# The attention scores' third product: both maps side by side, each in one half of the rows

## The chip, the cores and the metric

The kernel runs on one core of a Trainium2 chip. The metric is the device time of one execution in microseconds, as the median of several runs. The profile is one execution, recorded instruction by instruction. Five engines work in parallel, each through its own list in a fixed order: TensorE (PE, with its weight loads as PEld), VectorE (DVE), ScalarE (ACT), GpSimd (POOL) and SyncE (SP), which issues most transfers.

## The reference, cut to what matters

One layer of a hybrid encoder over 2048 tokens of width 1024: a combined input projection, differential attention and a gated delta rule as two branches, their gated merge, an output projection, and a mixture of experts. The change lies in the attention alone:

```python
DA_HEADS, DA_QK_DIM, DA_V_DIM = 4, 64, 128      # two maps of 64 channels per head
def probs(qm, km):
    s = jnp.einsum('bhqd,bhkd->bhqk', qm, km).astype(jnp.float32) * scale + bias
    return jax.nn.softmax(jnp.where(allowed, s, NEG_INF), axis=-1)
a = probs(qblk[..., 0, :], k1) - lam * probs(qblk[..., 1, :], k2)
return jnp.einsum('bhqk,bhkd->bhqd', a.astype(v.dtype), v)
```

So each head has two maps, and each map's scores contract over only 64 channels. `allowed` lets a query see the keys of its own chunk of 64 and of all chunks before it.

## The kernel before

Stages follow one another: conditioning and input projection (phase 1), the delta rule with the output gates, the attention with the branches' merge (phase 2), the output projection with routing (phase 3), the experts (phase 5). In most products each float32 operand is split into a high part that TensorE multiplies in its fast float32r form and a low part (what is left), so that a product takes three matmuls: high by high, high by low, low by high.

The attention goes by units `att(p, h, qt, ...)`: one head `h` and one tile of 128 queries `qt`, 64 units in three passes (`qt` 0 to 7, 8 to 11, 12 to 15). A unit does, for each of two maps `m` and each chunk `ch` of up to 512 keys:

- L979: queries' high part times keys. The contraction of 64 is doubled to 128 rows: the tile `K` holds a map's high keys in rows 0 to 63 and its low keys in rows 64 to 127, and `qd` holds the high queries twice. One matmul over 128 rows gives high by high plus high by low.
- L980: the third product, `ql` (the low queries, also held twice) times the same `K` tile, again over 128 rows, added in the same PSUM bank (tag `sc`, three banks).
- L982: VectorE reads the bank, adds the distance bias and keeps the minimum (tile `mx`), into the score rows `sp`.

After a map's chunks come the exponential on ScalarE (L987), and after both maps the combination (L994). Later come the transposes of the probabilities (`tr`, L1002), their copies (`aT`, L1004) and the products with the values (`av`, L1006).

The units are generators that `pipeline` starts one per turn; older ones go on to their next `yield 1`. Between the attention's units stand gate units (`pg`, L548 to L550, in the first pass) and merge units (`y`, L867 to L869). What order each engine runs comes from the framework's scheduler, which weaves these units together, so TensorE's list holds score products, transposes, value products and merge products in turn. The loads go through SyncE: `kv_load` (L946: per chunk one transfer for the high and one for the low keys, both maps in each; L948 for the values) and `q_load` (L956, L957: four transfers per head and 512 queries).

Of the kernel before, what the change touches and what calls it, by code (L numbers as in the profile page):

```python
# [9 lines left out]
F32 = mybir.dt.float32  # L10
F32R = mybir.dt.float32r
# [8 lines left out]
P = 128  # L20
# [23 lines left out]
# gates of the last slab that wait for the attention, and the units of it that they come before  # L44
# [16 lines left out]
def pipeline(units, old_first=False):  # L61
    """each turn starts a unit and runs the older ones to their next "yield 1"; "yield 0" lets the others in between"""
    active, more = [], True
    units = iter(units)
    while active or more:
        g = next(units, None)
        more = more and g is not None
        turn, active = ([] if g is None else [g]) + active, []
        if old_first:
            turn.reverse()  # L70
        while turn:
            again = []
            for g in turn:
                r = next(g, None)
                if r is not None:
                    (active if r else again).append(g)
            turn = again
        if old_first:
            active.reverse()


class K:
# [59 lines left out]
    # ---------------------------------------------------------------- phase 1  # L142
    def phase1(self, late):
# [13 lines left out]
        with ExitStack() as ctx:  # L157
# [25 lines left out]
            def load_x(p):  # L183
                """two tiles of x, normalized"""
# [7 lines left out]
                # the second pair is waited for: its first tile by itself  # L192
# [100 lines left out]
            # per-partition gain of q: both maps' 64 channels  # L293
# [7 lines left out]
            # a head's scores are in units of its slope, a power of two, until the bias is on  # L301
# [254 lines left out]
    def gates_and_gdn(self, ctx, sm, ps, hxp, hh, hl):  # L556
# [33 lines left out]
        # softplus(x) = max(x, 0) + log1p(e), e = exp(-|x|); log1p(e) = ln(u) e / (u - 1), u = 1 + e  # L590
# [96 lines left out]
        def scan(t):  # L687
# [6 lines left out]
            for b in range(4):  # L694
                pb, o = slice(32 * b, 32 * b + 32), 32 * (b % 2)
                nc.sync.dma_start(T[pb, :, o:o + 32], TB[t, :, b].rearrange("h r c -> r h c"))
                nc.sync.dma_start(U[pb, :, o:o + 32], UB[t, :, b].rearrange("h r c -> r h c"))
                # the zero quarter of each pair of blocks
                G.memset((U if b % 2 else T)[pb, :, 32 - o:64 - o], 0.0)
# [11 lines left out]
            # inverse of the unit triangular matrix, block doubling 32 -> 64 -> 128  # L711
# [32 lines left out]
            # recurrence over tiles of 128 tokens  # L744
# [76 lines left out]
    # ---------------------------------------------------------------- branch merge  # L821
    def merge_setup(self, ctx, ps):
# [6 lines left out]
        def load_o(s, n, h):  # L829
            """a head's output of a slab, as parts"""  # L830
            hi = c.tile([P, TS], F32R, tag="oh", name=f"h{n}{s}{h}", bufs=NOT)
            lo = c.tile([P, TS], F32R, tag="ol", name=f"l{n}{s}{h}", bufs=NOT)
            raw = lo.bitcast(F32)
            nc.sync.dma_start(raw, d[n][h, :, s * TS:(s + 1) * TS])
            A.copy(hi, raw)
            (V if s == NS - 1 else G).tensor_tensor(out=lo, in0=raw, in1=hi.bitcast(F32), op=ALU.subtract)
            ot[n, s, h] = hi, lo
# [47 lines left out]
    # ---------------------------------------------------------------- phase 2  # L885
    def phase2(self, cm, late):
# [3 lines left out]
        with ExitStack() as ctx:  # L890
# [8 lines left out]
            # ---- constants  # L899
# [16 lines left out]
            # distances of keys from queries, the last chunk's first half of queries doesn't see its second half of keys  # L916
# [9 lines left out]
            # ---- attention  # L926
            kv, qs = {}, {}

            def kv_tiles(p, h, n):
                """the first 512 keys' tiles come last: their memory is free first"""  # L930
# [6 lines left out]
            def kv_load(p, h, n):  # L937
                """the keys and values of a head, n chunks"""
# [4 lines left out]
                for s in range(n):  # L943
                    sl = slice(s * TS, (s + 1) * TS)
                    for j, nm in ((0, "k_hi"), (1, "k_lo")):
                        nc.sync.dma_start(Kt[s].bitcast(F32)[64 * j:64 * j + 64],  # L946
                                          d[nm][h].rearrange("(m p) t -> p m t", m=2)[:, :, sl])
                    nc.sync.dma_start(Vt[s], vs[:, 4 * s:4 * s + 4, :])  # L948

            def q_load(h, s):  # L950
                qd = ah.tile([P, 2, TS], F32R, tag="qd", bufs=NQ, name=f"qd{h}{s}")
                ql = ah.tile([P, 2, TS], F32R, tag="ql", bufs=NQ, name=f"ql{h}{s}")
                sl = slice(s * TS, (s + 1) * TS)
                for t, nm in ((qd, "q_hi"), (ql, "q_lo")):
                    src = d[nm][h].rearrange("(m p) t -> p m t", m=2)[:, :, sl]
                    nc.sync.dma_start(t.bitcast(F32)[0:64], src)  # L956
                    nc.sync.dma_start(t.bitcast(F32)[64:128], src)  # L957
                # numerators, their first maps' sums and sums of squares, of four query tiles
# [6 lines left out]
            def att(p, h, qt, sp_pool, w):  # L965
# [6 lines left out]
                sp = []  # L972
                for m in range(2):
                    b = sp_pool.tile([P, w], F32, tag="sp", name=f"sp{h}_{qt}_{m}")
                    mx = sm.tile([P, 5], F32, tag="mx", name=f"mx{h}_{qt}_{m}")
                    for ch in range(nch):
                        k0, n = ch * 512, min(512, nk - ch * 512)
                        pt = ps.tile([P, 512], F32, tag="sc", name=f"sc{h}_{qt}_{m}_{ch}", bufs=PSA[0])
                        PE.matmul(pt[:, :n], qd[:, m, q0], Kt[ch][:, m, 0:n], start=True, stop=False)  # L979
                        PE.matmul(pt[:, :n], ql[:, m, q0], Kt[ch][:, m, 0:n], start=False, stop=True)  # L980
                        mo = S - nk + k0
                        V.tensor_tensor_reduce(out=b[:, k0:k0 + n], in0=pt[:, :n], in1=Mt[:, mo:mo + n], op0=ALU.add,  # L982
                                               op1=ALU.min, scale=SLOPES[h], scalar=3e38, accum_out=mx[:, ch:ch + 1])
# [5 lines left out]
                    sp.append(b)  # L989
# [23 lines left out]
                # out = o / l1, rms-normalised; a mean square beyond float32 gives 0, as its rsqrt does  # L1013
# [27 lines left out]
            def units():  # L1041
# [14 lines left out]
                for i, (p, h, qt) in enumerate(todo):  # L1056
                    wn = TS * (p + 2)
                    if wn != w:
# [4 lines left out]
                        # the first pass's lies where the merge's tiles come, which are not to be loaded before  # L1063
# [31 lines left out]
    # ---------------------------------------------------------------- phase 3  # L1095
    def phase3(self, cm):
# [5 lines left out]
        with ExitStack() as ctx:  # L1102
# [72 lines left out]
            def outp(i, s, j):  # L1175
# [29 lines left out]
                # logits of a slab by columns: 36 rows of the weights' first parts, 36 of their second  # L1205
# [44 lines left out]
    # ---------------------------------------------------------------- phase 4  # L1250
    def route_consts(self, ctx):
# [3 lines left out]
        # descending weights 8..1, expert number, iota over slots columns and partitions  # L1255
# [14 lines left out]
        # an expert's share of the schedule, in half blocks: one, and one more for each of these its rank lies below  # L1270
# [17 lines left out]
    def first(self, sm, x, n, tg):  # L1288
        """one-hot of the first maximum over the last axis of x, and the maximum"""
# [16 lines left out]
    def route_a(self, sm, t0, t1):  # L1306
# [13 lines left out]
        # the two best experts of every group  # L1320
# [13 lines left out]
        # their weights  # L1334
# [10 lines left out]
    def route_b(self, c, sm, wk, wp, ps):  # L1345
# [8 lines left out]
        # loads of the experts, as a column and in every row  # L1354
# [6 lines left out]
        # positions of the assignments within their experts  # L1361
# [4 lines left out]
        # rank of an expert: experts in falling order of load, ties in expert order  # L1366
# [9 lines left out]
        # expert of a rank  # L1376
# [8 lines left out]
        # the schedule: NBLK blocks in rank order, what goes beyond an expert's share after them  # L1385
# [12 lines left out]
        # base, share and first further block of an expert in one number  # L1398
# [37 lines left out]
        # token and weight of a slot; the weight in two parts  # L1436
# [26 lines left out]
        # the other experts' weights are read after the first rows  # L1463
# [11 lines left out]
        # blocks beyond the schedule: how many, and each expert's range of them  # L1475
# [6 lines left out]
        def weights():  # L1482
# [5 lines left out]
            # halved, for the tanh form of silu  # L1488
# [5 lines left out]
    def spots(self, wk, wp, g, act=False):  # L1494
        """one-hot rows of the places in their blocks, of eight tiles of assignments"""
# [16 lines left out]
    def rows_of(self, pool, pt, nm):  # L1512
        """rows to gather and to add to, from a table of token numbers counted from 1, 0 where there is none"""
# [11 lines left out]
    # ---------------------------------------------------------------- phase 5  # L1525
    def phase5(self):
# [3 lines left out]
        with ExitStack() as ctx:  # L1530
# [15 lines left out]
            def chunks(e, i):  # L1546
                """loads of an expert's weights, two rows of 128 of w1 and w3 or one of w2 at a time"""
# [13 lines left out]
            def split(more):  # L1561
                """the next loaded weights' parts, and another load"""
# [14 lines left out]
            def block(i, more, gi, si, wt, nm):  # L1577
# [26 lines left out]
                # silu(a)*b, as a*(1 + tanh(a/2))*b/2; the half goes into the weight  # L1604
# [26 lines left out]
            def half(i, more, gi, si, wt, nm):  # L1631
                """a block of up to 64 tokens: their two parts side by side, the products with the first part of the
                weights in the upper and in the lower half, added afterwards"""
# [63 lines left out]
            def behind(g):  # L1697
                """the older block's products come before this one's rows"""
# [30 lines left out]
            with tc.For_i(0, n, 1) as i:  # L1729
                # the block's number, its expert, its tokens and their weights  # L1730
# [68 lines left out]
```

## Time and profile before

| | |
|---|---|
| median of 3 runs | 3081.26 us (3079.08 to 3086.68) |
| profiled execution, its span | 3079.4 us |
| TensorE busy over the span | 2844.8 us (92%) |
| attention stretch (first to last score product and its tail) | 1292 to 1824 us |
| TensorE busy in that stretch | 495.02 of 532 us |

The page gives no device time of the profiled execution other than its span, which lies 1.9 us below the median. A matmul's listed duration runs from its start to its last result and is longer than its share of the engine, since the next one starts before it has ended; so starts are compared with starts.

### The profile page before, as it was taken

Reading aid. Unit: us, or ns where it says so; the run is one execution under the profiler, and the core shown is the slowest. Engines: PE = TensorE matmul, PEld = TensorE weight load, DVE = VectorE, ACT = ScalarE, POOL = GpSimd, SP = SyncE. Lnnn points to the kernel's source line nnn. Section 1 sums busy time; section 2 is a strip of 40 time slices with the busy share of each in tenths; the row PEclk is TensorE's granted clock in tenths of the full one; section 3 lists DMA queues with packets and bytes.
Section 4 is the critical chain, followed back from the end, with each engine's and each line's share of the span. In section 5 each row is a group of like instructions: output and inputs, shape, how many; then the busy total and the mean of one; then the engine's idle time right before and its main releaser. Section 6 shows DMA issues by size and latency. Waiting matters only on the chain. (4 is left out here: it accounts for less than half of the span.)

```text
span 3079.4 us, 43963 instructions
## 1 busy us (share of the span) xinstructions
PE 2844.8 (92%) x14845; PEld 2294.6 (75%) x14845; DVE 2079.0 (68%) x4804; ACT 1332.7 (43%) x2409; POOL 837.8 (27%) x614
## 2 busy tenths in 40 slices
PE   6999999999999999999899999997799899999897
PEld 4888778777877777777788787786577677667675
DVE  7567669985276443377757655676867767886876
ACT  4512223333322333377555543221545545554554
POOL 2200000000221222001342324221544545543553
PEclk9999999999999999999999999998799999999998
DMA  6334652221554664585676647532978888886895
GB/s 224 119 86 117 202 182 80 79 67 53 165 144 130 185 179 147 149 200 148 167 179 171 168 110 235 195 144 103 324 240 259 260 258 292 294 291 217 271 312 148
DMA packets 426245, 561.20 MB, mean 182 GB/s; under 512 B 56520, under 2 KB 240920, under 8 KB 426016
## 3 DMA queue, kind: packets, MB, share of 16 engines
q1 hardware_dynamic: 340560, 440.87, 46.4%
q10 hardware_dynamic: 73744, 75.53, 7.3%
q0 software_dynamic: 11712, 41.95, 5.8%
q8 instruction: 119, 1.95, 0.3%
q14 instruction: 110, 0.90, 0.1%
HBM read 436.06 MB, written 122.18 MB: 181 GB/s over the span
## 5 line engine op out<-in xcount | busy, mean ns | idle before, releaser
L1570 DVE TENSOR_TENSOR low<-raww,hiw 128x1024 fp32r<-128x1024 f32 x288 | 434.4, 1554 | 46.8 <-ACT hiw L1568 44.2
L1568 ACT CAST hiw<-raww 128x1024 fp32r<-128x1024 f32 x384 | 378.8, 1048 | 153.6 <-PE py L1624 67.7
L1570 POOL TENSOR_TENSOR low<-raww,hiw 128x1024 fp32r<-128x1024 f32 x96 | 263.2, 2771 | 118.9 <-ACT hiw L1568 112.7
L982 DVE CUSTOM_DVE_ANT_0 sp<-sc,M 128x512 f32<-128x512 f32 (+1 forms) x320 | 183.6, 604 | 53.1 <-PE sc L980 52.0
L548 PE MATMUL pg<-hh,ghi 128*128 128x512 f32 x512 | 210.5, 411 | 2.5 <-ACT ghi L539 2.5
L332 PE MATMUL mma<-whi,hh 128*128 128x512 f32 x512 | 208.5, 407 | 2.4 <-ACT hh L248 1.0
L550 PE MATMUL pg<-hh,glo 128*128 128x512 f32 x512 | 208.3, 407 | 0.0
L549 PE MATMUL pg<-hl,ghi 128*128 128x512 f32 x512 | 208.0, 406 | 0.0
L334 PE MATMUL mma<-whi,hl 128*128 128x512 f32 x512 | 202.8, 396 | 0.6 <-DVE hl L249 0.6
L333 PE MATMUL mma<-wlo,hh 128*128 128x512 f32 x512 | 202.1, 395 | 0.4 <-DVE wlo L255 0.4
L987 ACT ACTIVATE sp<-sp,mx 128x128 f32<-128x128 f32 (+15 forms) x128 | 153.7, 1201 | 46.4 <-DVE mx L985 40.7
L1006 PEld LDWEIGHTS av<-V,aT 128*128 128x128 f32 x1088 | 140.2, 196 | 34.6 <-ACT aT L1004 26.7
L1006 PE MATMUL av<-V,aT 128*128 128x128 f32 x1088 | 151.6, 284 | 13.9 <-ACT aT L1004 12.7
L255 POOL TENSOR_TENSOR wlo<-raw,whi 128x512 fp32r<-128x512 f32 x12 | 16.9, 1428 | 533.0 <-ACT whi L254 533.0
L342 PE MATMUL mmb<-hh,whi 128*128 128x512 f32 x384 | 155.3, 404 | 5.4 <-ACT whi L254 5.4
L344 PE MATMUL mmb<-hh,wlo 128*128 128x512 f32 x384 | 151.1, 393 | 0.6 <-POOL wlo L255 0.4
L343 PE MATMUL mmb<-hl,whi 128*128 128x512 f32 x384 | 150.3, 391 | 0.0
L979 PE MATMUL sc<-K,qd 128*128 128x512 f32 (+1 forms) x320 | 132.1, 416 | 14.7 <-DVE mx L982 10.9
L1623 PE MATMUL py<-hiw,dh 128*128 128x512 f32 x272 | 115.1, 423 | 20.4 <-ACT dh L1614 20.3
L1597 PE MATMUL pb<-low,xh 128*128 128x512 f32 x272 | 112.7, 414 | 18.3 <-DVE low L1570 10.7
L1579 POOL DMA_INDIRECT x<-h,sgi x34 | 63.6, 1872 | 230.1 <-PE tx L1586 132.7
L1597 PE MATMUL pa<-low,xh 128*128 128x512 f32 x272 | 111.3, 409 | 11.9 <-DVE low L1570 11.9
(555 smaller groups left out, 7522.3 us busy)
## 6 DMA issues: line engine op xcount, KB each, us to landing
raww<-in_w_dram SPq DMA_DIRECT2D x384, 512.0 KB
mw<-in_w_ada_dram SPq DMA_DIRECT2D x64, 256.0 KB
gate<-gt ACTq DMA_DIRECT2D x64, 256.0 KB
g<-gate SPq DMA_DIRECT2D x64, 256.0 KB
graw<-in_w_in_dram SPq DMA_DIRECT2D x52, 256.0 KB
raw<-in_w_in_dram SPq DMA_DIRECT2D x22, 512.0 KB
K<-k_hi SPq DMA_DIRECT2D x36, 256.0 KB
K<-k_lo SPq DMA_DIRECT2D x36, 256.0 KB
```

The lines of the kernel that those rows point to most:

```text
L332: nc.tensor.matmul(pt[:, :n], a, his[k][:, :n], start=(k == 0), stop=False)
L333: nc.tensor.matmul(pt[:, :n], a, los[k][:, :n], start=False, stop=False)
L334: nc.tensor.matmul(pt[:, :n], b, his[k][:, :n], start=False, stop=(k == KT - 1))
L342: nc.tensor.matmul(pt, a, hh[s][:, k, :], start=(k == 0), stop=False)
L548: nc.tensor.matmul(pt, hi[:, k, :], hh[:, k, :], start=(k == 0), stop=False)
L549: nc.tensor.matmul(pt, hi[:, k, :], hl[:, k, :], start=False, stop=False)
L550: nc.tensor.matmul(pt, lo[:, k, :], hh[:, k, :], start=False, stop=(k == KT - 1))
L982: V.tensor_tensor_reduce(out=b[:, k0:k0 + n], in0=pt[:, :n], in1=Mt[:, mo:mo + n], op0=ALU.add, op1=ALU.min, scale=SLOPES[h], scalar=3e38, ...
L1006: PE.matmul(av[:, :P], aT[:, k * P:(k + 1) * P], Vt[k4 // 4][:, k, :], start=(k4 + k == 0), stop=(k4 + k == qt))
L1568: A.copy(hi, raw)
L1570: on.tensor_tensor(out=lo, in0=raw, in1=hi.bitcast(F32), op=ALU.subtract)
L1597: PE.matmul(p_, xh[:, k, :], w[i, n, k][q], start=(k == 0 and q == 0), stop=False)
```

## The change

The keys' tile is laid out anew: for map 0 the high keys stand in rows 0 to 63 and the low ones in rows 64 to 127, as before; for map 1 the high keys stand in rows 64 to 127 and the low ones in rows 0 to 63. The low queries are held once, map 0 in rows 0 to 63 and map 1 in rows 64 to 127. The third product is then a matmul over 64 rows: low queries by high keys alone, the upper rows for map 0, the lower rows for map 1 (low by low is left out of the sum). The two maps of a chunk are emitted together: both first products, both third products, both VectorE passes. Both maps' exponentials stand after the last chunk. Each key transfer is split by map, and the low queries need one transfer in place of two. Comments were removed from the file, so that lines behind the change stand about six lower: L980 and L984 are now the first and third product, L987 the VectorE pass, L1008 and L1012 the transposes and value products.

```diff
                 for s in range(n):
                     sl = slice(s * TS, (s + 1) * TS)
-                    for j, nm in ((0, "k_hi"), (1, "k_lo")):
-                        nc.sync.dma_start(Kt[s].bitcast(F32)[64 * j:64 * j + 64],
-                                          d[nm][h].rearrange("(m p) t -> p m t", m=2)[:, :, sl])
+                    for m in range(2):
+                        for j, nm in ((m, "k_hi"), (1 - m, "k_lo")):
+                            nc.sync.dma_start(Kt[s].bitcast(F32)[64 * j:64 * j + 64, m, :],
+                                              d[nm][h, 64 * m:64 * m + 64, sl])
...
-                ql = ah.tile([P, 2, TS], F32R, tag="ql", bufs=NQ, name=f"ql{h}{s}")
+                ql = ah.tile([P, TS], F32R, tag="ql", bufs=NQ, name=f"ql{h}{s}")
...
+                nc.sync.dma_start(ql.bitcast(F32), d["q_lo"][h][:, sl])
...
-                sp = []
+                sp = [sp_pool.tile([P, w], F32, tag="sp", name=f"sp{h}_{qt}_{m}") for m in range(2)]
+                mxs = [sm.tile([P, 5], F32, tag="mx", name=f"mx{h}_{qt}_{m}", bufs=6) for m in range(2)]
+                for ch in range(nch):
+                    k0, n = ch * 512, min(512, nk - ch * 512)
+                    pts = [ps.tile([P, 512], F32, tag="sc", name=f"sc{h}_{qt}_{m}_{ch}", bufs=PSA[0]) for m in range(2)]
+                    for m, pt in enumerate(pts):
+                        PE.matmul(pt[:, :n], qd[:, m, q0], Kt[ch][:, m, 0:n], start=True, stop=False)
+
+                    for m, pt in enumerate(pts):
+                        r = slice(64 * m, 64 * m + 64)
+                        PE.matmul(pt[:, :n], ql[r, q0], Kt[ch][r, m, 0:n], start=False, stop=True)
+                    mo = S - nk + k0
+                    for m, pt in enumerate(pts):
+                        V.tensor_tensor_reduce(out=sp[m][:, k0:k0 + n], in0=pt[:, :n], in1=Mt[:, mo:mo + n], op0=ALU.add,
+                                               op1=ALU.min, scale=SLOPES[h], scalar=3e38, accum_out=mxs[m][:, ch:ch + 1])
                 for m in range(2):
-                    b = sp_pool.tile([P, w], F32, tag="sp", name=f"sp{h}_{qt}_{m}")
-                    mx = sm.tile([P, 5], F32, tag="mx", name=f"mx{h}_{qt}_{m}")
-                    for ch in range(nch):
-                        k0, n = ch * 512, min(512, nk - ch * 512)
-                        pt = ps.tile([P, 512], F32, tag="sc", name=f"sc{h}_{qt}_{m}_{ch}", bufs=PSA[0])
-                        PE.matmul(pt[:, :n], qd[:, m, q0], Kt[ch][:, m, 0:n], start=True, stop=False)
-                        PE.matmul(pt[:, :n], ql[:, m, q0], Kt[ch][:, m, 0:n], start=False, stop=True)
...
+                    b, mx = sp[m], mxs[m]
```

TensorE's list in the third pass before the change, at query tile 13 of the third head (a row reads line, operation, output tile with query tile, map and chunk in its name, then stationary and moving operand in the trace's order, and the size):

```order
L979 MATMUL sc_13_0_0_17119<-K_16332,qd_16346 128x512
L980 MATMUL sc_13_0_0_17119<-K_16332,ql_16347 128x512
L979 MATMUL sc_13_0_1_17123<-K_16326,qd_16346 128x512
L980 MATMUL sc_13_0_1_17123<-K_16326,ql_16347 128x512
L979 MATMUL sc_13_0_2_17127<-K_16328,qd_16346 128x512
L980 MATMUL sc_13_0_2_17127<-K_16328,ql_16347 128x512
L1002 MATMUL tr_12_0_17162<-ident,sp_12_0_16955 128x128 x3
L979 MATMUL sc_13_0_3_17131<-K_16330,qd_16346 128x256
L980 MATMUL sc_13_0_3_17131<-K_16330,ql_16347 128x256
```

The same place after the change:

```order
L980 MATMUL sc_13_0_0_17177<-K_16374,qd_16396 128x512
L980 MATMUL sc_13_1_0_17178<-K_16374,qd_16396 128x512
L984 MATMUL sc_13_0_0_17177<-K_16374,ql_16397 128x512
L984 MATMUL sc_13_1_0_17178<-K_16374,ql_16397 128x512
L980 MATMUL sc_13_0_1_17185<-K_16368,qd_16396 128x512
L984 MATMUL sc_13_0_1_17185<-K_16368,ql_16397 128x512
L1008 MATMUL tr_12_0_17218<-ident,sp_12_0_17011 128x128 x2
L980 MATMUL sc_13_1_1_17186<-K_16368,qd_16396 128x512
L984 MATMUL sc_13_1_1_17186<-K_16368,ql_16397 128x512
L1008 MATMUL tr_12_0_17218<-ident,sp_12_0_17011 128x128 x2
```

Only the first chunk's two third products (L984) stand next to each other. From the second chunk on, each stands alone, with transposes or the other map's first product behind it. Over the whole list the 320 third products form 259 groups without another product between them: 199 of one, 59 of two and one of three, so that 60 of the 160 pairs stand together; the 60 hold 27,520 of the 69,632 columns that one map's third products have in all. Behind 108 of the groups stands a 512-wide or narrower float32r product, behind 151 a transpose or value product.

SyncE's list at the first head's loads, before and after the change (a piece of the difference, names of buffers kept):

```order
L956 DMA qd_12033<-q_hi 64x2x512
L957 DMA qd_12033<-q_hi 64x2x512
L956 DMA ql_12034<-q_lo 64x2x512
L957 DMA ql_12034<-q_lo 64x2x512
L946 DMA K_12031<-k_hi 64x2x512
L946 DMA K_12031<-k_lo 64x2x512
```

The low queries' two transfers become one of 128 rows (L959), and each key transfer becomes two of half the size (L948 in the new file).

## Rows read from the trace of the kernel before

**Rows 1.** The page's head and busy times: engine, busy us (share of the span), instructions.

```profile
span 3079.4 us, 43963 instructions
PE 2844.8 (92%) x14845; PEld 2294.6 (75%) x14845; DVE 2079.0 (68%) x4804; ACT 1332.7 (43%) x2409; POOL 837.8 (27%) x614
```

**Rows 2.** Busy time by stretch, the attention: us, each engine's busy us (instructions), clock.

```profile
core 0: us, PE busy (x) PEld busy (x) DVE busy (x) ACT busy (x) POOL busy (x), PEclk, DMA share, GB/s
1292.00:1824.00 532.00, 495.02 (x2920) 416.01 (x2921) 375.09 (x1267) 322.02 (x701) 130.38 (x103) 0.97 0.66 167
```

**Rows 3.** Instruction groups of TensorE in 1292 to 1824: busy, mean | idle before, releasers.

```profile
L1006 PE MATMUL av<-V,aT 128*128 128x128 f32 x1034 | 144.7, 285 | 13.9 <-ACT aT L1004 12.7 <-ACT av L1009 0.9
L979 PE MATMUL sc<-K,qd 128*128 128x512 f32 (+1 forms) x320 | 132.1, 416 | 14.7 <-DVE mx L982 10.9 <-DMA qd<-q_hi 1.5 <-DMA K<-k_lo 0.9
L980 PE MATMUL sc<-K,ql 128*128 128x512 f32 (+1 forms) x320 | 119.5, 380 | 2.1 <-DMA ql<-q_lo 2.1
```

**Rows 4.** TensorE in order of time, attention: start, duration, line, operation, rows*columns, size.

```profile
1704.90 0.39 PE L980 MATMUL sc<-K,ql 128*128 128x512 f32 x1
1705.13 0.38 PE L1002 MATMUL tr<-ident,sp 128*128 128x128 f32 x2
1705.27 0.48 PE L979 MATMUL sc<-K,qd 128*128 128x512 f32 x1
1705.58 0.40 PE L980 MATMUL sc<-K,ql 128*128 128x512 f32 x1
```

**Rows 5.** TensorE in order of time, delta rule: eight 64-row products among gate products.

```profile
1070.95 0.40 PE L550 MATMUL pg<-hh,glo 128*128 128x512 f32 x1
1071.28 0.68 PE L737 MATMUL p<-sU,nw 64*64 64x64 f32 x8
1071.88 0.50 PE L548 MATMUL pg<-hh,ghi 128*128 128x512 f32 x1
1072.22 0.40 PE L549 MATMUL pg<-hl,ghi 128*128 128x512 f32 x1
```

**Rows 6.** TensorE in order of time, experts: four 64-row transposes, four 128-row ones behind them.

```profile
2268.91 0.40 PE L1599 MATMUL pb<-hiw,xl 128*128 128x512 f32 x1
2269.24 0.46 PE L1674 MATMUL th<-ident,ha 64*128 64x64 f32 x4
2269.64 0.66 PE L1586 MATMUL tx<-ident,x 128*128 128x128 f32 x4
2270.05 0.48 PE L1597 MATMUL pa<-hiw,xh 128*128 128x512 f32 x1
2270.37 0.39 PE L1597 MATMUL pa<-low,xh 128*128 128x512 f32 x1
```

**Rows 7.** TensorE in order of time, experts: 128-row products that use half of the columns.

```profile
2238.90 0.40 PE L1657 MATMUL pb<-hiw,xh 128*128 128x512 f32 x1
2239.13 0.39 PE L1657 MATMUL pa<-low,xh 128*64 128x512 f32 x1
2239.37 0.39 PE L1657 MATMUL pb<-low,xh 128*64 128x512 f32 x1
```

**Rows 8.** TensorE in order of time, delta rule: 32-row products in different parts of the array.

```profile
951.67 0.19 PE L724 MATMUL pb<-A,sT 32*32 32x32 f32 x1
951.68 0.19 PE L717 MATMUL pa<-sU,nw 32*32 32x32 f32 x1
951.68 0.19 PE L726 MATMUL pb<-sT,A 32*32 32x32 f32 x1
951.71 0.19 PE L724 MATMUL pb<-A,sT 32*32 32x32 f32 x1
```

**Rows 9.** Instruction groups of VectorE in 1292 to 1824, by shape, columns as above.

```profile
L982 DVE CUSTOM_DVE_ANT_0 sp<-sc,M 128x512 f32<-128x512 f32 x224 | 147.9, 684 | 29.6 <-PE sc L980 29.0
L982 DVE DVE_READ_ACCUMULATOR2_ANT mx<- 128x1 f32 x320 | 26.1, 81 | 0.0
```

**Rows 10.** Waits of VectorE in 1292 to 1830: who for whom, us, times, longest.

```profile
DVE cf L992 <- ACT sp L987: 44.1, 27, 2.5
```

**Rows 11.** The key loads' line on SyncE: count, duration ns (min/median/max), first and last start.

```profile
L946 SPq DMA_DIRECT2D K<-k_hi x36: 573/586/1631, 1284.8 to 1763.8; - x36
L946 SPq DMA_DIRECT2D K<-k_lo x36: 574/605/807, 1285.4 to 1764.4; - x36
```

More of the change, by code (lines that the diff above doesn't have):

```diff
@@ L951, in q_load @@
                 qd = ah.tile([P, 2, TS], F32R, tag="qd", bufs=NQ, name=f"qd{h}{s}")
-                ql = ah.tile([P, 2, TS], F32R, tag="ql", bufs=NQ, name=f"ql{h}{s}")
+                ql = ah.tile([P, TS], F32R, tag="ql", bufs=NQ, name=f"ql{h}{s}")
                 sl = slice(s * TS, (s + 1) * TS)
[L954 to L957, printed above, removed]
+                src = d["q_hi"][h].rearrange("(m p) t -> p m t", m=2)[:, :, sl]
+                nc.sync.dma_start(qd.bitcast(F32)[0:64], src)
+                nc.sync.dma_start(qd.bitcast(F32)[64:128], src)
+                nc.sync.dma_start(ql.bitcast(F32), d["q_lo"][h][:, sl])
                 ob = at.tile([P, 4, P], F32, tag="ob", bufs=4, name=f"ob{h}{s}")
@@ L971, in att @@
                 nch = (nk + 511) // 512
-                sp = []
-                for m in range(2):
-                    b = sp_pool.tile([P, w], F32, tag="sp", name=f"sp{h}_{qt}_{m}")
-                    mx = sm.tile([P, 5], F32, tag="mx", name=f"mx{h}_{qt}_{m}")
-                    for ch in range(nch):
-                        k0, n = ch * 512, min(512, nk - ch * 512)
-                        pt = ps.tile([P, 512], F32, tag="sc", name=f"sc{h}_{qt}_{m}_{ch}", bufs=PSA[0])
-                        PE.matmul(pt[:, :n], qd[:, m, q0], Kt[ch][:, m, 0:n], start=True, stop=False)
-                        PE.matmul(pt[:, :n], ql[:, m, q0], Kt[ch][:, m, 0:n], start=False, stop=True)
-                        mo = S - nk + k0
-                        V.tensor_tensor_reduce(out=b[:, k0:k0 + n], in0=pt[:, :n], in1=Mt[:, mo:mo + n], op0=ALU.add,
-                                               op1=ALU.min, scale=SLOPES[h], scalar=3e38, accum_out=mx[:, ch:ch + 1])
+                sp = [sp_pool.tile([P, w], F32, tag="sp", name=f"sp{h}_{qt}_{m}") for m in range(2)]
[12 more added lines that the diff above has]
+                                               op1=ALU.min, scale=SLOPES[h], scalar=3e38, accum_out=mxs[m][:, ch:ch + 1])
+                for m in range(2):
+                    b, mx = sp[m], mxs[m]
                     if nch > 1:
@@ L988, in att @@
                                  accum_out=(l1, l2)[m][:, j:j + 1])
-                    sp.append(b)
                 yield 1
```

## The prediction

> **What bounds the kernel now.** I read the page first: TensorE is busy for 92% of the span and no other engine for more than 68% [rows 1]. Then the busy times by stretch: in the attention, the only place where the change acts, TensorE is busy for 495.0 of 532 us at a granted clock of 0.97 of full speed, VectorE for 375.1, and so 37 us of TensorE are idle [rows 2]. The groups of that stretch say where: 13.9 us before the value products, mostly for ScalarE's copies, 14.7 us before the first score product, of which 10.9 for VectorE to empty a bank, 2.1 for a load of queries [rows 3]. So TensorE's list, run in order, sets the stretch's length, and a price or gain on TensorE reaches the end nearly in full, except where it falls into those 37 us.
>
> The timeline gives the prices. A 512-wide float32r product is followed by the next instruction 0.23 us later (1704.90 to 1705.13). Two transposes and a first score product behind it take from 1705.13 to 1705.58, 0.45 us, so a 128-wide transpose costs 0.11. From one L980 to the next it is 0.68 us, which is 0.23 + 2 x 0.11 + 0.23: weaving transposes between score products costs nothing today [rows 4].
>
> **What the change takes away.** Two third products of one chunk in different halves of the rows could run at once. The trace has no pair of 64-row products like that. The nearest rows are the delta rule's 32-row ones: three products in different parts of the array start within 0.01 us, while the same line returns 0.04 us later [rows 8]. So I take side by side as true where the two follow each other directly, a gain of one product's time for the pair. But TensorE's list after the change has only 60 of 160 pairs standing together; in the other 100 a transpose, a value product or the other map's first product stands between, and TensorE runs its list in order. The 60 pairs hold 27,520 columns, which is 53.75 products of 512 at 0.23: **12.4 us taken away** (0 if they do not overlap). A third product that stands alone over 64 rows is as wide as before and saves nothing.
>
> **What the change adds on TensorE.** Every group of third products is now a visit to 64 rows among products over 128 rows, and the trace shows what such a visit costs. In [rows 5] the time from L550's start to the second product behind the visit is 1072.22 - 1070.95 = 1.27 us. The work in it is 0.23 for L550, eight 64-wide products at 0.06 (half of the 0.11 of a 128-wide one, rounded up) and 0.23 for L548: 0.94. The visit cost 0.33 us over its work: 0.10 to get in (0.33 between L550 and L737 where 0.23 is usual), about 0.10 to get out and 0.11 more on the first product behind (0.34 to the next), the rest inside. In [rows 6] it is the same with 64-row transposes and 128-row transposes behind them: 2270.37 - 2268.91 = 1.46 us, less 0.23 + 4 x 0.06 + 4 x 0.11 + 0.23 = 1.14, leaves 0.32. No idle time is listed before any of these rows; nothing is waited for. It is the rows, not the columns: products that use 64 columns and all 128 rows follow the others at 0.23 and 0.24 [rows 7], and 128-row transposes cost nothing extra [rows 4].
>
> The Trainium skill says in "TensorEngine Tiling (Array Packing)", Key Properties, that changing the tiling mode, and not just the tile within one, drains TensorE. By that, every visit drains twice, as [rows 5, 6] show; that columns alone change without any delay [rows 7] it does not separate. The page gives no duration.
>
> No row shows a 512-wide 64-row product in such a visit. From below: only the way in, 0.10 us [rows 5]. From above: the first product of the visit also starts as slowly as the first one behind it, 0.11 more, but without what was lost inside in [rows 5]: 0.40. I take 0.33, since in both kinds of visit seen, with float32r products and with transposes behind, it comes out at 0.33 and 0.32. The list after the change has 259 groups: 259 x 0.33 = **85.5 us added** (26 to 104).
>
> **What hides some of it.** Where TensorE waits today, a slower TensorE waits less: at most the 37 us of [rows 2]. In the dense parts VectorE offers no cover: a chunk takes it 0.684 + 0.081 = 0.77 us [rows 9], while TensorE's share of a chunk goes from 0.68 [rows 4] to 0.68 + 0.33 = 1.01. And the waits for loads and for the first chunks of a unit stay. I take a third, **12 us** (0 to 37).
>
> **Edits costed at nothing.** Both exponentials now stand at the unit's end, so the combination waits longer for ScalarE; VectorE waits 44.1 us there today [rows 10], and the cover is the next unit's or merge's products on TensorE, which need none of it. If that cover were gone, at most the length of one such wait, 2.5 us, would fall on a unit. Both score rows are claimed at the unit's start, the second one up to four chunks (3 us) sooner; no wait for them is among the waits of today. SyncE issues 72 more key transfers and 16 fewer query transfers of 0.6 us each [rows 11], 34 us over a stretch of 532, most in bursts of 4 to 8 more transfers per head, 2.4 to 4.8 us; heads are loaded one ahead, and TensorE waits 0.9 us for keys today [rows 3]. Only the first head is not loaded ahead: 2 key issues more and 1 query issue less before its first chunk, under 1 us, while gate products still run. VectorE's and ScalarE's work is the same in count and size.
>
> **Sum.** -12.4 + 85.5 - 12 = +61 us. On the profiled span of 3079.4 that is 3140; the median lies 1.9 above that span, so I predict **3142 us**, 2% slower, all of it within the attention stretch, which grows from 532 to about 593 us. What follows starts later and is otherwise as before.
>
> **Rivals.**
> 1. *The visit is cheap for these products*, because a 512-wide product gives the engine time to get the next weights ready, and just the way in of 0.10 us stays: +26 - 12.4 = +13.5 us, about 3095. For it: the rows inside the visits of [rows 5, 6] are short ones. Against: the delay behind the visit is seen on 512-wide products with 512-wide ones following.
> 2. *Faster.* The visit costs nothing, and pairs overlap. It gives -12.4 us, about 3069, as the list stands; it decides below a price of 12.4 / 259 = 0.048 us a visit, and to be faster by 9 us (0.3%, about what a measurement of this kernel can tell from no change) below 0.013. For it: [rows 8]. Against: 0.10 in on every visit seen, before any other part. If all 160 pairs overlapped and no visit cost anything it would be 69,632 columns, 136 products x 0.23 = -31 us, about 3050; the list excludes it. The Trainium skill's page "TensorE: Matmul & The Clock Gate", Part 3, lets products in distinct row groups run at once, some 4 ns apart, which is this case for the pairs that stand together.
> 3. *Worse.* The pairs do not overlap, the visit costs 0.40 and nothing is hidden: +104, about 3185. For it: no 64-row pair is in the trace. Against: TensorE's waits must shrink somewhat.
> 4. *The waits hide much more:* all 37 us vanish: +85.5 - 12.4 - 37 = +36, about 3117. For it: the waits for the copies and banks are those a slower TensorE loses. Against: [rows 9], and loads.
>
> **Chances.** The forecast with its own range, 3125 to 3180: 0.64. Rival 4's end, 3105 to 3125: 0.14. Rival 1, 3090 to 3105: 0.06. Rival 3, above 3180: 0.05. No change within 0.3%, a visit of about 0.05 us: 0.06. Rival 2: 0.05. So slower has 0.89, the same 0.06, faster 0.05. The range of 3102 to 3178 leaves out rivals 1 to 3 and no change, about 0.2.
>
> **What would show it.** In the profile after: from a first score product's start to the third product behind it 0.33 us and not 0.23; behind a lone third product some 0.3 and more to the next but one; in pairs that stand together the second third product within 0.02 us of the first; TensorE's share of the attention up by about 73 us, its idle time down, VectorE waiting longer for L984 than its 29.0 us for L980 in [rows 9]. The prediction is wrong if third products follow first products at 0.23, or if the stretch does not grow.

## The result and the profile after

The changed kernel takes 3133.17 us (median of 4 runs, 3126.86 to 3137.60) where the kernel before takes 3083.97 (median of 4): **slower by 1.64%** (ratio 1.0164, 95% interval 1.0148 to 1.0179), some 50 us. 3142 was forecast, with a range of 3102 to 3178.

The page's head and busy times after:

```profile
span 3135.9 us, 44025 instructions
PE 2923.8 (93%) x14845; PEld 2289.3 (73%) x14845; DVE 2096.2 (67%) x4804; ACT 1333.6 (43%) x2409; POOL 854.0 (27%) x614
```

The span grew by 56.5 us and TensorE's busy time by 79.0, with 14,845 products recorded in both [rows 1]. The attention stretch (columns as in [rows 2]), and TensorE's and VectorE's groups in it:

```profile
1293.00:1882.00 589.00, 576.40 (x2936) 415.48 (x2936) 388.37 (x1266) 320.91 (x700) 147.12 (x103) 0.96 0.54 146
```

```profile
L1012 PE MATMUL av<-V,aT 128*128 128x128 f32 x1030 | 152.8, 292 | 3.9 <-ACT aT L1010 2.8 <-ACT av L1015 1.0
L980 PE MATMUL sc<-K,qd 128*128 128x512 f32 (+3 forms) x320 | 134.2, 446 | 5.4 <-DVE mx L987 3.6 <-DMA K<-k_lo 1.6
L984 PE MATMUL sc<-K,ql 64*128 64x512 f32 (+3 forms) x319 | 124.0, 479 | 0.0
...
L987 DVE CUSTOM_DVE_ANT_0 sp<-sc,M 128x512 f32<-128x512 f32 x223 | 148.3, 686 | 65.9 <-PE sc L984 59.1 <-PE tr L1008 5.9
```

From the first score product to the last it is 586.8 us (1293.6 to 1880.4) where it was 530.0 (1292.3 to 1822.3): 57 us more, which is the whole growth of the span. TensorE is idle for 12.6 us of the stretch and was for 37.0 [rows 2]. The waits before the value products fell from 13.9 to 3.9 us and those before the first product from 14.7 to 5.4 [rows 3], while VectorE now waits 59.1 us for the third product where it waited 29.0 [rows 9]: TensorE fell behind its neighbours. The third product's mean duration went from 380 to 479 ns.

TensorE in order of time, one chunk with its pair together and two chunks with lone third products (L1008 are transposes):

```profile
1746.81 0.40 PE L869 MATMUL y<-hoTA,wlw_branch_a 128*128 128x512 f32 x1
1747.04 0.62 PE L980 MATMUL sc<-K,qd 128*128 128x512 f32 x2
1747.59 0.50 PE L984 MATMUL sc<-K,ql 64*128 64x512 f32 x2
1748.02 0.49 PE L980 MATMUL sc<-K,qd 128*128 128x512 f32 x1
1748.44 0.49 PE L984 MATMUL sc<-K,ql 64*128 64x512 f32 x1
1748.87 0.44 PE L1008 MATMUL tr<-ident,sp 128*128 128x128 f32 x2
1749.06 0.48 PE L980 MATMUL sc<-K,qd 128*128 128x512 f32 x1
1749.47 0.50 PE L984 MATMUL sc<-K,ql 64*128 64x512 f32 x1
1749.90 0.44 PE L1008 MATMUL tr<-ident,sp 128*128 128x128 f32 x2
```

Two things are to be seen. The pair at 1747.59 lasts 0.50 us for both, as long as a lone third product does (0.49, 0.50): the two run at once. And the visit is dear: two first products take 0.55 until the third begins (1747.04 to 1747.59) where two steps of 0.23 are 0.46; the pair takes 0.43 until the next product (to 1748.02) where one product takes 0.23. From one lone third product to the next, with a transposes' pair between, it is 1749.47 - 1748.44 = 1.03 us; the same work took 0.68 in [rows 4]. **A lone third product costs 0.35 us more than it did.**

The weight loads show where the time goes. First the load for the last third product of [rows 4], before the change, then a first and a lone third product after it:

```profile
1705.35 0.19 PEld L980 LDWEIGHTS sc<-K,ql 128*128 128x128 f32 x1
```

```profile
1749.03 0.19 PEld L980 LDWEIGHTS sc<-K,qd 128*128 128x128 f32 x1
1749.47 0.18 PEld L984 LDWEIGHTS sc<-K,ql 64*128 64x128 f32 x1 [0.25 <-issue]
```

Before, the weights of the third product begin to load 0.23 us ahead of it (1705.35, the product at 1705.58), while the first product still runs. After, the load and the product start together (1749.47), behind 0.25 us in which no wait is listed. Over all 320 third products the median lead was 228 ns and is 2 ns. So a visit loses the lead of the weights; that this is its whole price is not shown.

### The profile page after: what moved, and what is told of

Its sections match the earlier page's. It is cut to its first block, busy times and chain, and to the rows that moved or that the text cites. A ratio compares the mean times of both kernels' runs of the same rounds, so it can differ in the third digit from the quotient of the medians.

```text
span 3135.9 us, 44025 instructions
## 1 busy us (share of the span) xinstructions
PE 2923.8 (93%) x14845; PEld 2289.3 (73%) x14845; DVE 2096.2 (67%) x4804; ACT 1333.6 (43%) x2409; POOL 854.0 (27%) x614
## 5 line engine op out<-in xcount | busy, mean ns | idle before, releaser
L987 DVE CUSTOM_DVE_ANT_0 sp<-sc,M 128x512 f32<-128x512 f32 (+3 forms) x320 | 188.1, 607 | 93.3 <-PE sc L984 86.0
L1012 PE MATMUL av<-V,aT 128*128 128x128 f32 x1088 | 160.5, 291 | 3.9 <-ACT aT L1010 2.8
L1012 PEld LDWEIGHTS av<-V,aT 128*128 128x128 f32 x1088 | 139.9, 198 | 30.5 <-ACT aT L1010 15.2
L980 PE MATMUL sc<-K,qd 128*128 128x512 f32 (+3 forms) x320 | 134.2, 446 | 5.4 <-DVE mx L987 3.6
L1010 ACT COPY aT<-tr 128x512 f32<-128x512 f32 (+3 forms) x160 | 79.0, 519 | 131.2 <-PE tr L1008 131.1
```

Source lines behind the costliest of these rows:

```text
L987: V.tensor_tensor_reduce(out=sp[m][:, k0:k0 + n], in0=pt[:, :n], in1=Mt[:, mo:mo + n], op0=ALU.add, op1=ALU.min, scale=SLOPES[h], scalar=3 ...
L1012: PE.matmul(av[:, :P], aT[:, k * P:(k + 1) * P], Vt[k4 // 4][:, k, :], start=(k4 + k == 0), stop=(k4 + k == qt))
```

## The experiments

Ratios are against runs of the kernel before that were taken beside each, with 95% intervals; a difference in us is one of the medians.

**All rows again, everything else kept** (`e1_full_rows`). The third product goes back to 128 rows, so low by low is in the sum again:

```diff
...
-                nc.sync.dma_start(ql.bitcast(F32), d["q_lo"][h][:, sl])
+                src = d["q_lo"][h].rearrange("(m p) t -> p m t", m=2)[:, :, sl]
+                nc.sync.dma_start(ql.bitcast(F32)[0:64], src)
+                nc.sync.dma_start(ql.bitcast(F32)[64:128], src)
...
-                        PE.matmul(pt[:, :n], ql[r, q0], Kt[ch][r, m, 0:n], start=False, stop=True)
+                        PE.matmul(pt[:, :n], ql[:, m, q0], Kt[ch][:, m, 0:n], start=False, stop=True)
```

> The changed kernel with its third product over all 128 rows again: the low queries are held twice, so low by low is back in the sum; the keys' layout and split transfers, the two maps emitted together and the late exponentials stay, and TensorE's list has the same 259 groups of third products (200 of one, 57 of two, 2 of three). Theory A (each visit to 64 rows costs TensorE about 0.36 us, which is 56.8 us of growth plus 24.6 us of idle time used up plus 12.4 us of overlap, over 259): the loss goes away, 3076 to 3092 us. Rival B (the loss comes from the new order, the late exponentials or the split transfers): it stays near 3133 us; a share of it that stays is theirs.

Measured: 3077.92 us, ratio 0.9992 (0.9982 to 1.0002). The loss is gone. TensorE in order of time (L982 is the first product, L985 the third, L1013 value products):

```profile
1702.98 0.48 PE L982 MATMUL sc<-K,qd 128*128 128x512 f32 x1
1703.29 0.39 PE L985 MATMUL sc<-K,ql 128*128 128x512 f32 x1
1703.52 0.38 PE L1013 MATMUL av<-V,aT 128*128 128x128 f32 x2
1703.66 0.47 PE L982 MATMUL sc<-K,qd 128*128 128x512 f32 x1
1703.97 0.39 PE L985 MATMUL sc<-K,ql 128*128 128x512 f32 x1
```

The third product's step is 0.23 again (1703.29 to 1703.52), a chunk 0.68, and the median lead of the third product's weights 227 ns. So the new order, the two maps' emission, the late exponentials and the 72 further key transfers cost nothing together; the 64 rows cost it all. What each of those does alone was not run.

**No pairs** (`e2_map_by_map`): the maps one after the other, with the 64-row third product.

```diff
-                for ch in range(nch):
-                    k0, n = ch * 512, min(512, nk - ch * 512)
-                    pts = [ps.tile([P, 512], F32, tag="sc", name=f"sc{h}_{qt}_{m}_{ch}", bufs=PSA[0]) for m in range(2)]
+                for m in range(2):
...
+                    for ch in range(nch):
...
                         PE.matmul(pt[:, :n], qd[:, m, q0], Kt[ch][:, m, 0:n], start=True, stop=False)
...
                         PE.matmul(pt[:, :n], ql[r, q0], Kt[ch][r, m, 0:n], start=False, stop=True)
```

> The changed layout and the 64-row third product, but the maps emitted one after the other as before the change: no pair stands together, TensorE's list has 318 groups (317 of one). Theory A: 318 x 0.36 = 115 us, no overlap, 25 to 35 us of today's idle time used up: +80 to +90 over before, 3163 to 3175 us, slower than the change itself. Rival B (the emission of both maps together is at fault): back near 3083 us. Rival C (a visit is dear only with a pair in it): between, below 3120 us.

Measured: 3151.82 us, ratio 1.0238 (1.0223 to 1.0253), +73 us. Slower than the change, as theory A has it, though 7 to 17 us less than it said. Rival B and C fall. The stretch (columns as in [rows 2]):

```profile
1289.00:1897.00 608.00, 605.76 (x2941) 429.34 (x2942) 387.43 (x1267) 328.04 (x703) 131.66 (x103) 0.97 0.52 141
```

TensorE's idle time is used up: 2.2 of 608 us are left. What was too high is theory A's price of 0.36, which holds the loss at the lower clock as well (see below). With 0.32, 318 visits are 102 us; less 35 of idle time used up, and with some 7 more lost at the lower clock, that is 74, where 73 was measured.

**Pairs held together** (`e3_pairs_together`) and **the same in the same rows** (`e4_pairs_same_rows`). In the first, both third products are queued behind both first ones:

```diff
-                        PE.matmul(pt[:, :n], qd[:, m, q0], Kt[ch][:, m, 0:n], start=True, stop=False)
+                        first = PE.matmul(pt[:, :n], qd[:, m, q0], Kt[ch][:, m, 0:n], start=True, stop=False)
...
+                    with tc.issue_after(first.ins):
+                        for m, pt in enumerate(pts):
+                            r = slice(64 * m, 64 * m + 64)
+                            PE.matmul(pt[:, :n], ql[r, q0], Kt[ch][r, m, 0:n], start=False, stop=True)
```

In the second besides `r = slice(0, 64)` for both maps, with the keys laid out as before the change.

> The changed kernel with both third products of a chunk queued behind both first products: 166 groups in place of 259 (154 of two, 12 of one). Theory A: 166 x 0.36 = 60 us, less 30 us of overlap, less 15 to 25 us of idle time used up: +5 to +15 over before, 3088 to 3099 us. Rival D (a visit's price grows with the products in it, or pairs don't overlap): 3115 us or more. If visits were free: 3055 us.

> As the run with pairs together, but both maps' third products use the upper 64 rows (keys laid out as before the change, low queries of both maps in rows 0 to 63): 163 groups, 157 of two, which can't overlap. Theory A with overlap worth 0.23 us for a pair of 512: 27 to 32 us slower than the run with pairs together, 3115 to 3130 us. If the overlap is worth nothing: the same as that run.

Measured: 3103.65 us, ratio 1.0078 (1.0061 to 1.0096), +25, for the first; 3123.65, ratio 1.0140 (1.0125 to 1.0155), +45, for the second. Fewer visits cost less, but the first is 10 to 20 us above what theory A gave it over before, and still slower than before. The second is 20 us slower, where 27 to 32 were expected. In the second one's order of time (L981 first products, L986 third):

```profile
1708.55 0.62 PE L981 MATMUL sc<-K,qd 128*128 128x512 f32 x2
1709.10 0.73 PE L986 MATMUL sc<-K,ql 64*128 64x512 f32 x2
1709.76 0.50 PE L981 MATMUL sc<-K,qd 128*128 128x512 f32 x1
1710.09 0.60 PE L1010 MATMUL tr<-ident,sp 128*128 128x128 f32 x4
```

Two third products in the same rows take 0.73 us in all and 0.66 until the next product (1709.10 to 1709.76). Side by side they took 0.50 and 0.43 in the changed kernel. The overlap is worth 0.23 us a pair, one product's time, as the prediction had it.

Part of what the first of the two lost is no visit's price. Its TensorE in order of time, the end of a VectorE pass in the same place, and TensorE in the second run:

```profile
1705.21 0.60 PE L1009 MATMUL tr<-ident,sp 128*128 128x128 f32 x4
1705.73 0.50 PE L980 MATMUL sc<-K,qd 128*128 128x512 f32 x1
```

```profile
1705.60 0.08 DVE L988 DVE_READ_ACCUMULATOR2_ANT mx<- 128x1 f32 x1
```

```profile
1726.28 0.60 PE L1010 MATMUL tr<-ident,sp 128*128 128x128 f32 x4
1726.64 0.47 PE L981 MATMUL sc<-K,qd 128*128 128x512 f32 x1
```

Four transposes and the way to the first product take 0.52 us in the first run and 0.36 in the second. In the first, the product starts 0.05 us after VectorE has ended its read of the minimum (1705.68): it waited for a bank. No idle time is listed, since the transposes' listed time reaches to 1705.81. At full clock 41 first products behind 128-wide ones start so, 8.4 us later in all than with the usual step of 0.03 us; in the second run it is 4 and 0.5 us, in the changed kernel 3 and 0.6, before it 5 and 1.0. Without these waits the difference of 20 would be 28, within the 27 to 32 that were expected.

**A visit by itself** (`e5_tiny_64_rows`) and its control (`e6_tiny_128_rows`). The kernel before, with one small product more ahead of each first score product, over 64 rows or over all; its result is overwritten:

```diff
+                        PE.matmul(pt[:, :64], qd[0:64, m, q0], Kt[ch][0:64, m, 0:64], start=True, stop=True)
                         PE.matmul(pt[:, :n], qd[:, m, q0], Kt[ch][:, m, 0:n], start=True, stop=False)
```

> The kernel before with one small product more ahead of each first score product: 64 rows, 64 columns wide, into the bank that the first product then overwrites; 320 visits to 64 rows, nothing else changed, and TensorE's list is row for row that of the run with the same small product over 128 rows. Theory A (the price is that of getting into 64 rows and out, whatever stands inside): 320 x about 0.32 us more than that control, less some 25 us of idle time used up: 65 to 90 us above the control. Rival C (the price comes with a 512-wide product of half the rows, or with pairs): within 20 us of the control.

> The control: the same 320 small products over all 128 rows. Each is 0.03 us wide and leaves no time to load the next weights behind it, so up to 0.1 us each: +5 to +25 us over before, by every theory.

Measured: 3191.72 us, ratio 1.0338 (1.0317 to 1.0360); the control 3122.98, ratio 1.0121 (1.0104 to 1.0138). The visits cost 69 us above the control, theory A; the control itself cost more than expected. In order of time, first with 64 rows (L979 is the small product, L981 the third), then the control:

```profile
1709.44 0.39 PE L981 MATMUL sc<-K,ql 128*128 128x512 f32 x1
1709.76 0.29 PE L979 MATMUL sc<-K,qd 64*128 64x64 f32 x1
1709.99 0.50 PE L980 MATMUL sc<-K,qd 128*128 128x512 f32 x1
1710.32 0.39 PE L981 MATMUL sc<-K,ql 128*128 128x512 f32 x1
```

```profile
1717.23 0.40 PE L981 MATMUL sc<-K,ql 128*128 128x512 f32 x1
1717.47 0.19 PE L979 MATMUL sc<-K,qd 128*128 128x64 f32 x1
1717.50 0.48 PE L980 MATMUL sc<-K,qd 128*128 128x512 f32 x1
1717.81 0.40 PE L981 MATMUL sc<-K,ql 128*128 128x512 f32 x1
```

From one third product to the next it is 0.88 us with the visit and 0.58 without: 0.30 for the same columns, on the same engine, in the same order. The delay comes in three places, as in [rows 5]: 0.32 to get in (0.24 in the control), 0.23 until the first product behind (0.03), 0.33 on that product (0.31 in the control too). The control's 0.11 us per small product (medians of 0.577, and 0.463 in the kernel before), over 320, makes 36 of its 39 us.

**Four together** (`e7_four_together`) and its control (`e8_banks_control`): the third products of two chunks behind all four first ones, with `PSA = (12, 6, 5), (4, 1, 1)`; the control is the kernel before with that last setting.

> The changed kernel with the third products of two chunks together (four in one stay), which takes four banks for scores and leaves one for the transposes in place of two: 117 groups (46 of four, 11 of three, 43 of two, 17 of one). Theory A: 117 x 0.35 = 41 us less about 30 us of overlap less idle time used up: within 5 us of its bank control, so faster than pairs held together against before, if the banks cost nothing. If the price grows with the products inside: 20 us or more above the control.

> The kernel before with four banks for scores and one for transposes in place of three and two: what the banks alone do to the run with four together. 3075 to 3095 us by every theory: transposes and their copies can no longer overlap, but merge products stand between.

Measured: 3098.51 us, ratio 1.0044 (1.0027 to 1.0061), and the control 3080.50, ratio 0.9995 (0.9985 to 1.0006). Four to a visit lose 14 us against before, less than pairs, but are 18 us above the control, where at most 5 was expected. The visits of four do what they should:

```profile
1718.12 1.09 PE L982 MATMUL sc<-K,qd 128*128 128x512 f32 x4
1719.14 0.73 PE L986 MATMUL sc<-K,ql 64*128 64x512 f32 x4
1719.81 0.44 PE L1011 MATMUL tr<-ident,sp 128*128 128x128 f32 x2
```

Four third products take 0.67 us until the next (two pairs at 0.23 and 0.21 to get out). Only 46 of the 117 visits hold four, though, and TensorE is idle for about as long as in the control (33 us and 32, the listed waits summed), so nothing of the price is hidden.

**Visits elsewhere** (`e9_fewer_visits`, `e10_full_square`). The price is paid in the kernel before too, in the delta rule [rows 5]. Its two 64-row products got zeros for the other rows, and in the second kernel all 128 columns as well (columns that nothing reads). The edits of the first of the two products, from the kernel before to the first kernel, and from that to the second:

```diff
-                PE.matmul(p3[0:64, h * 64:(h + 1) * 64], nl[64:128, h, 0:64], U[64:128, h, :], start=True, stop=True)
+                PE.matmul(p3[0:64, h * 64:(h + 1) * 64], nl[:, h, 0:64], W[:, h, 64:128], start=True, stop=True)
...
-                PE.matmul(p3[0:64, h * 64:(h + 1) * 64], nl[:, h, 0:64], W[:, h, 64:128], start=True, stop=True)
+                PE.matmul(p3[:, h * 64:(h + 1) * 64], nl[:, h, :], W[:, h, 64:128], start=True, stop=True)
```

> The kernel before, attention untouched, with 32 other visits to fewer rows taken away: the delta rule's two 64-row products per tile of 128 tokens (L737 and L741) run over 128 rows, their other half of the contraction filled with zeros that GpSimd writes; the products' widths and the output stay. Theory A: 32 x about 0.33 us, 11 us faster on TensorE in the delta-rule stretch, where it is busy for 95% of the time: 6 to 12 us faster, ratio 0.996 to 0.998. If the price of a visit there is hidden by waits, or the added copies on GpSimd lie in the way: no change.

> As the run with fewer visits, but the delta rule's two products also use all 128 columns (the weights' next 64 columns are taken along and their results not read). In that run the stretch kept its 342 us, and its products over 128 rows and 64 columns in plain float32 still had 0.33 ahead of them where 0.23 is usual, and 0.11 more behind. Theory A2 (a float32 product of less than the whole square is a visit too, by rows or by columns): the visits go now, 29 x 0.33 = 9.6 us, 3068 to 3077 us, ratio 0.996 to 0.998. Rival (the delay belongs to this place, a change of kind of product or a wait that the trace doesn't show): no change again.

Measured: 3081.79 us, ratio 1.0008 (0.9994 to 1.0022), and 3085.58, ratio 1.0014 (0.9996 to 1.0032): no gain from either, where 6 to 12 us and some 10 were expected by theory A and A2. In order of time, first with 128 rows and 64 columns, then with the full square:

```profile
953.59 0.39 PE L549 MATMUL pg<-hl,ghi 128*128 128x512 f32 x1
953.91 0.68 PE L739 MATMUL p<-nw 128*64 128x64 f32 x8
954.52 0.50 PE L550 MATMUL pg<-hh,glo 128*128 128x512 f32 x1
954.85 0.40 PE L548 MATMUL pg<-hh,ghi 128*128 128x512 f32 x1
```

```profile
953.06 0.40 PE L549 MATMUL pg<-hl,ghi 128*128 128x512 f32 x1
953.30 1.00 PE L741 MATMUL p<-nw 128*128 128x64 f32 x8
954.11 0.48 PE L550 MATMUL pg<-hh,glo 128*128 128x512 f32 x1
954.42 0.40 PE L548 MATMUL pg<-hh,ghi 128*128 128x512 f32 x1
```

With all rows and 64 columns the eight products are a visit as before: 0.32 in, 0.33 behind, 1.26 us in all (1.27 in [rows 5]). With the full square the visit is gone (0.24 in, 0.31 behind), but the eight take 0.81 us, most of them 0.11 apart where they were 0.06 apart with 64 columns: 1.36 in all. So theory A2's visit went and another price came; which part of the square's weights makes the 0.11 was not taken apart.

No version tried beats the kernel before.

## Why the prediction was right

**The visit's price** was taken as 0.33 us. I summed all steps from one TensorE start to the next in the attention, each against the usual step of its kind (0.231 us for 512 columns, 0.109 for a 128-wide transpose or value product), with time at the lower clock counted half and idle time kept apart. The steps into, out of and right behind third products hold 106.0 us of delay after and 22.9 before: 83.1 us, 0.32 for each of 259 visits. 85.5 was forecast. The runs show that it is the rows: with the same 259 groups over 128 rows nothing is lost (`e1_full_rows`), and a 64-column product of 64 rows costs 0.30 more than one of 128 (`e5_tiny_64_rows`). That the price is of that kind for a 512-wide product, for which no row stood before, is shown by 1.03 against 0.68 us.

The Trainium skill's sentence in "TensorEngine Tiling (Array Packing)", Key Properties, that a change of tiling mode drains TensorE, agrees with these runs where the rows change; the price here is 0.30 to 0.35 us for the way there and back.

**The overlap** was taken as 12.4 us for 60 pairs. The second third product starts 3 ns after the first (median of the pairs), and the same sum gives 12.2. The Trainium skill's "TensorE: Matmul & The Clock Gate", Part 3, has 4 ns for products in distinct row groups; this trace agrees. `e4_pairs_same_rows` shows it from the other side.

**What hides it** was the term that was mis-sized. A third of the idle 37 us was taken, 12; its idle time between the first and the last score product fell from 36.6 to 12.0, 24.6. Nearly every wait for ScalarE's copies and VectorE's banks went, since TensorE came later than they did.

**The edits costed at nothing** cost nothing: together 0.9992 in `e1_full_rows`. VectorE's combination waited 49.9 us for the exponentials where it had waited 44.1 [rows 10], the longest 5.0 where the prediction had 2.5; `e1_full_rows`, with the same late exponentials, shows that it did not lengthen the run.

**What was not in the sum**: the profiled execution after has 44 us of the stretch at the lower of the two clocks (1.2 GHz) and the one before 27 (granted clock 0.96 and 0.97 over the stretch); half of the 17 us difference, 8.5, is lost, as an estimate. That the visits bring this on is not shown: the same figure is 41 with 318 lone visits and 55 for pairs in the same rows, but 27 for pairs together, 14 in `e1_full_rows`, and 41 in `e6_tiny_128_rows`, which has no visits, one execution each.

The sum so far is 83.1 - 12.2 - 24.6 + 8.5 = 54.8 of 57 us in the profiled executions; where the other 2 us went is open. The medians differ by 49, since the profiled execution after was its slowest of four and the one before not. That the forecast came within 9 us is in part luck: 12.6 us too little hidden and 8.5 us of clock left out offset each other in part.

**A reading of the prediction that does not hold**: "No idle time is listed before any of these rows; nothing is waited for." The 41 waits in `e3_pairs_together` are not listed either. That the visits' delays are no such waits is shown by `e5_tiny_64_rows` against its control.

**Rivals.** Rival 1 and 2 need a visit near 0.10 or below 0.05, and fall by `e5_tiny_64_rows`. Rival 3 falls by the overlap seen. Rival 4 was half right: more was hidden than I took, but not all, and its 3117 lies below every run after.

**Open**: a part of the 10 to 20 us by which `e3_pairs_together` was slower than expected. Its idle time (21 us) and its overlap (30 us) came out as expected, so its balance gives about 0.41 us for each of 166 visits (23 growth of the span, 15 of idle time used, 30 of overlap). Without the 8 us of unlisted waits for banks it is 0.36, still a little above the 0.32 of the changed kernel, and no run tells why.

## What to carry to other kernels

Count the times that TensorE's list goes from full-array products to products of half the rows and back: here each costs 0.30 to 0.35 us, more than the 0.23 that a pair of 512 columns gains. By these prices a visit must hold at least two pairs to gain anything (an estimate: 2 x 0.23 against 0.35), and the list as the scheduler makes it must keep them together; no run here gained, also not the one with 46 such visits among 117. Read that list, not the loop in the source. Before a packing is tried, look whether the kernel already has such products somewhere: their rows give the price. And idle time that a profile lists is not all the waiting there is: compare a product's start with the end of what it depends on.

## What the runs showed of the hardware that was not expected

- Columns alone are free in one case and not in another. Float32r products of 128 rows and 64 columns, 512 wide, follow full ones at 0.23 us [rows 7]; plain float32 products of 128 rows and 64 columns cost the whole visit, 0.32 in and 0.33 behind (`e9_fewer_visits`). So the prediction's sentence "It is the rows, not the columns" does not hold for every product. The two cases differ in type and also in width (512 and 64); which of them decides was not run.
- A 64-wide float32 product takes 0.06 us with 64-column weights and 0.11 with 128-column weights (`e10_full_square`): for a group of eight that is more than the visit's price.
- A 64-column product put between two 512-wide ones costs 0.11 us though its own step is 0.03 (`e6_tiny_128_rows`); the product behind it takes 0.31.
